# Prefix log-sum-exp in place: an fp32 work tile in three column chunks, row sums on VectorE, one fp32 product per chunk, and a range check

## The chip, the cores and the metric

The kernel runs on one core of one Trainium2 chip. The metric is the device time of one execution in microseconds (us). TensorE, VectorE, ScalarE and GpSimd appear in the profile as PE, DVE, ACT and POOL; SP is the engine that issues all transfers between DRAM and the core's memory (SBUF). PEld is TensorE's weight load, and a trailing q (SPq) means the engine's queue.

## The reference

The input x is a float32 array of 4 batches x 4096 rows x 4128 columns, drawn from a standard normal distribution. For each batch and each column the output is the running log-sum-exp down the rows:

```python
out[:, 0, :] = x[:, 0, :].copy()
for t in range(1, S):
    mx = np.maximum(out[:, t - 1, :], x[:, t, :])
    out[:, t, :] = mx + np.log(np.exp(out[:, t - 1, :] - mx) + np.exp(x[:, t, :] - mx))
```

So row t holds the logarithm of the sum of exp(x) over rows 0 to t. 270.5 MB are read and as many written.

## The kernel before

A **step** takes 128 x r consecutive rows of one batch, with r = 3 (or 2 where the 32 groups of 128 rows of a batch don't divide by three). Partition p holds rows p*r to p*r+r-1, so a step is one contiguous transfer of r rows per partition. There are 44 steps: 11 per batch, the step with r = 2 first in batch 0 and last in batches 1 to 3. Four work tiles (`xpool`, 4 buffers of 3 x 4128 float32 per partition) hold the steps. `Step.load` (L132) and `Step.store` (L135) are issued by SP and nothing else is; the result is written into the same work tile over the input.

A step is cut into 4 **chunks** of 1024 columns; the last chunk also carries the 32 columns that are left over, with small products and tiles of their own (`tail_head`, `qt`). What happens to a chunk:

- `exp` (L147, ACT) computes exp of its r rows as fp16, packed over the input's place in the work tile;
- `later` (L155, DVE) adds rows 1 and 2 into a float32r tile `sum`;
- `head` (PE) builds in PSUM the running sum at row 0 of each partition: an inclusive triangular product of row 0, an exclusive triangular product of the others (L167 for the float32r sum), and a `pick` product that adds the total of the step before out of `carry`;
- `stage(j)` takes the logarithm of PSUM into row j of the work tile (L198, ACT), then an identity product adds row j+1 to PSUM;
- after the last row `keep` (L111 and L112, DVE) saves the total as a high and a low fp16 part in `carry`.

The order of instructions on every engine is the order of the program text (`manual_schedule`), an order written out by hand. In turn g of the main loop the kernel issues `later` of chunk g+1, then the stages of chunks g-2, g-1 and g, then `exp` of chunk g+2 and `head` of chunk g+1. When the last stage of a step's last chunk is issued, SP gets that step's store and, right behind it, the load three steps ahead, which has to wait until the store before has left its tile:

```python
                if k.c == last and d + 1 == k.t.r:
                    k.t.store()
                    if bufs <= stored + ahead < len(steps):
                        steps[stored + ahead].load()
                    stored += 1
```

Of the kernel before, what the change touches and what calls it, by code (L numbers as in the profile page):

```python
# [6 lines left out]

FP32 = mybir.dt.float32
FP16 = mybir.dt.float16
FP32R = mybir.dt.float32r  # L10
ACT = mybir.ActivationFunctionType
P = 128
R = 3
CH = 1024
MM = 512
HI, LO = 96, 32


def _constants(nc, pool):


    def tri(base, name):
        t = pool.tile([P, P], FP16, name=name)
        nc.gpsimd.memset(t, 1.0)

        nc.gpsimd.affine_select(
            out=t, in_=t, pattern=[[1, P]], compare_op=mybir.AluOpType.is_ge,
            fill=0.0, base=base, channel_multiplier=-1,
        )
        return t  # L30

    def ones_where_zero(bases, step, name):
        t = pool.tile([P, P], FP16, name=name)
        nc.gpsimd.memset(t, 0.0)
        for base in bases:
            nc.gpsimd.affine_select(
                out=t, in_=t, pattern=[[step, P]], compare_op=mybir.AluOpType.not_equal,
                fill=1.0, base=base, channel_multiplier=1,
            )
        return t  # L40

    return (
        tri(0, "incl"),
        tri(-1, "excl"),
        ones_where_zero([0], -1, "ident"),
        ones_where_zero([-(HI + 31), -(LO + 31)], 0, "pick"),
    )


@with_exitstack  # L50
def kernel(
# [2 lines left out]
    x: bass.AP,  # L54
    out: bass.AP,
):

    nc = tc.nc
    B, S, D = x.shape
    assert S % P == 0
    n_main = D // CH
    tail = D - n_main * CH
    t0 = n_main * CH
    last = n_main - 1

    nc.scalar.preload_act_table_set("natural_log_exp_and_others")
    consts = ctx.enter_context(tc.tile_pool(name="consts", bufs=1))
    incl, excl, ident, pick = _constants(nc, consts)

    bufs = 4
    xpool = ctx.enter_context(tc.tile_pool(name="xpool", bufs=bufs))
    cpool = ctx.enter_context(tc.tile_pool(name="cpool", bufs=1))
    pmain = ctx.enter_context(tc.tile_pool(name="pmain", bufs=3, space=bass.MemoryType.PSUM))
    ptail = ctx.enter_context(tc.tile_pool(name="ptail", bufs=2, space=bass.MemoryType.PSUM))

    carry = [cpool.tile([P, CH], FP16, name=f"carry{c}") for c in range(n_main)]
    carry_t = cpool.tile([P, tail], FP16, name="carry_t")
    for t in (*carry, carry_t):
        nc.vector.memset(t, 0.0)

    spool = ctx.enter_context(tc.tile_pool(name="spool", bufs=1))
    excl_r = consts.tile([P, P], FP32R, name="excl_r")
    nc.vector.tensor_copy(excl_r, excl)

    ctx.enter_context(tc.manual_schedule())  # L90

    held = [None]

    def mm(pt, w, rhs, start=False, stop=False):

        if held[0] is not w:
            nc.tensor.matmul(pt, lhsT=w, rhs=rhs, start=start, stop=stop, skip_group_check=True)  # L97
            held[0] = w
            return
        pe = nc.tensor  # L100
        pe.add_instruction(mybir.InstMatmult(  # L101
            name=nc.get_next_instruction_name(),
            ins=[pe.lower_ap(rhs), pe.lower_ap(w, for_matmul_weights=True)],
            outs=[pe.lower_ap(pt, opt=True)],
            start_tensor_calc=start, stop_tensor_calc=stop, ldweights=False,
            tile_size=(P, P), tile_position=(0, 0), bass_skip_group_check=True,
        ))

    def keep(cr, pt):

        nc.vector.tensor_copy(cr[HI:HI + 32, :], pt[HI:HI + 32])  # L111
        nc.vector.tensor_tensor(  # L112
            out=cr[LO:LO + 32, :], in0=pt[HI:HI + 32], in1=cr[HI:HI + 32, :],
            op=mybir.AluOpType.subtract,
        )

    class Step:


        def __init__(self, b, row, r):  # L120
            self.b, self.row, self.r = b, row, r
            self.first = row == 0

        def dram(self, t):
            rows = t[self.b, self.row:self.row + P * self.r, :]
            return rows.rearrange("(p j) d -> p j d", j=self.r)

        def load(self):
            full = xpool.tile([P, R, D], FP32, name="xt")
            self.xt = full[:, :self.r, :]  # L130
            self.half = self.xt.bitcast(FP16)
            nc.sync.dma_start(out=self.xt, in_=self.dram(x))  # L132

        def store(self):
# [1 line left out]

    class Chunk:
        def __init__(self, step, c):
            self.t, self.c = step, c
            self.w = D - last * CH if c == last else CH  # L140

        def e(self, j, a, b):
            return self.t.half[:, j, 2 * self.c * CH + a:2 * self.c * CH + b]

        def exp(self):
            c0, w = self.c * CH, self.w
            nc.scalar.activation(  # L147
                self.t.half[:, :, 2 * c0:2 * c0 + w], self.t.xt[:, :, c0:c0 + w], ACT.Exp,
            )

        def later(self):

            if self.t.r == 3:
                self.sum = spool.tile([P, CH], FP32R, name="sum")
                nc.vector.tensor_tensor(  # L155
                    out=self.sum, in0=self.e(1, 0, CH), in1=self.e(2, 0, CH),
                    op=mybir.AluOpType.add,
                )

        def head(self):  # L160
            t = self.t
            pt = self.pt = pmain.tile([P, CH], FP32, name="pt")
            for s in range(0, CH, MM):
                mm(pt[:, s:s + MM], incl, self.e(0, s, s + MM), start=True)
            if t.r == 3:
                for s in range(0, CH, MM):
                    nc.tensor.matmul(  # L167
                        pt[:, s:s + MM], lhsT=excl_r, rhs=self.sum[:, s:s + MM],
                        start=False, stop=False, skip_group_check=True,
                    )  # L170
                held[0] = None
            else:
                for s in range(0, CH, MM):
                    mm(pt[:, s:s + MM], excl, self.e(1, s, s + MM))
            if not t.first:
                for s in range(0, CH, MM):
                    mm(pt[:, s:s + MM], pick, carry[self.c][:, s:s + MM])
            if self.c == last:
                self.tail_head()

        def tail_head(self):


            t, r = self.t, self.t.r
            full = ptail.tile([P, R, tail], FP32, name="qt")
            qt = self.qt = full[:, :r, :]
            to = lambda v, n: v.unsqueeze(1).to_broadcast([P, n, tail])
            for i in range(r):
                mm(qt[:, i:, :], incl, to(self.e(i, CH, CH + tail), r - i), start=i == 0)
            for i in range(1, r):  # L190
                mm(qt[:, :i, :], excl, to(self.e(i, CH, CH + tail), i))
            if not t.first:
                mm(qt, pick, to(carry_t, r))

        def stage(self, j):

            t, c, pt = self.t, self.c, self.pt
            nc.scalar.activation(t.xt[:, j, c * CH:(c + 1) * CH], pt, ACT.Ln)  # L198
            if j + 1 < t.r:
                for s in range(0, CH, MM):  # L200
                    mm(pt[:, s:s + MM], ident, self.e(j + 1, s, s + MM), stop=j + 2 == t.r)
                if c == last and j == 0:
                    nc.scalar.activation(t.xt[:, :, t0:D], self.qt, ACT.Ln)  # L203
                    keep(carry_t, self.qt[:, t.r - 1, :])
            else:
                keep(carry[c], pt)

    steps = []
    for b in range(B):
        n = S // P  # L210
        parts = [R] * (n // R) + ([n % R] if n % R else [])
        if b == 0:
            parts.reverse()
        row = 0
        for r in parts:
            steps.append(Step(b, row, r))
            row += P * r
        assert row == S

    chunks = [Chunk(s, c) for s in steps for c in range(n_main)]  # L220
    ahead = bufs - 1
    for s in steps[:bufs]:
        s.load()
    stored = 0
    chunks[0].exp()
    chunks[1].exp()
    chunks[0].later()
    chunks[0].head()
    for g in range(len(chunks) + R - 1):
        if g + 1 < len(chunks):  # L230
            chunks[g + 1].later()
        for d in range(R - 1, -1, -1):
            if 0 <= g - d < len(chunks) and d < chunks[g - d].t.r:
                k = chunks[g - d]
                k.stage(d)
                if k.c == last and d + 1 == k.t.r:
                    k.t.store()
                    if bufs <= stored + ahead < len(steps):
                        steps[stored + ahead].load()
                    stored += 1  # L240
        if g + 2 < len(chunks):
            chunks[g + 2].exp()
        if g + 1 < len(chunks):
            chunks[g + 1].head()


# [28 lines left out]
```

## Time and profile before

| | |
|---|---|
| time, median of 3 runs | 1262.85 us (1262.8 to 1263.05) |
| span of the profiled execution | 1261.5 us |
| busy: PE / DVE / ACT | 661.2 / 647.7 / 947.3 us (52% / 51% / 75%) |
| DMA | 541.44 MB, mean 429 GB/s over the span |
| mean granted TensorE clock | 0.722 |
| ACT waiting for a load (L147) | 248.4 us |

The profiled execution is listed with its span, from the first to the last instruction; the 1.35 us by which the median time is longer lie around the span. "Busy" is a share of the whole span. A group of instructions is listed with its count, its busy time, the mean duration of one in ns, and the idle time of the engine before it with what ended that idle time. Windows list busy time per engine in a stretch of the span, then the granted clock, the share of the 16 DMA engines' time in use, and GB/s.

### The profile page before, as it was taken

Reading aid. Unit: us, or ns where it says so; the run is one execution under the profiler, and the core shown is the slowest. Engines: PE = TensorE matmul, PEld = TensorE weight load, DVE = VectorE, ACT = ScalarE, POOL = GpSimd, SP = SyncE. Lnnn points to the kernel's source line nnn. Section 1 sums busy time; section 2 is a strip of 40 time slices with the busy share of each in tenths; the row PEclk is TensorE's granted clock in tenths of the full one; section 3 lists DMA queues with packets and bytes.
Section 4 is the critical chain, followed back from the end, with each engine's and each line's share of the span. In section 5 each row is a group of like instructions: output and inputs, shape, how many; then the busy total and the mean of one; then the engine's idle time right before and its main releaser. Section 6 shows DMA issues by size and latency. Waiting matters only on the chain. (4 is left out here: it accounts for less than half of the span.)

```text
span 1261.5 us, 5926 instructions
## 1 busy us (share of the span) xinstructions
PE 661.2 (52%) x1948; PEld 236.7 (19%) x1948; DVE 647.7 (51%) x606; ACT 947.3 (75%) x733; POOL 2.2 (0%) x13
## 2 busy tenths in 40 slices
PE   3655545465555555555446554555534655544562
PEld 1222111122121111211112121111111221111120
DVE  2674445554555545545446545544544645544454
ACT  5997777777777777778669777777866977777784
POOL 0000000000000000000000000000000000000000
PEclk9987676766577776768757677766775767787666
DMA  9999999999999999999999999999999999999998
GB/s 410 410 437 434 429 430 437 431 430 431 440 430 431 430 439 430 431 433 431 438 433 435 428 432 438 432 430 431 434 435 430 435 427 436 434 434 429 437 416 346
DMA packets 12702, 541.44 MB, mean 429 GB/s; under 512 B 1408, under 2 KB 1408, under 8 KB 1408
## 3 DMA queue, kind: packets, MB, share of 16 engines
q1 hardware_dynamic: 12672, 541.07, 99.4%
q8 instruction: 15, 0.25, 0.1%
q14 instruction: 15, 0.12, 0.0%
HBM read 270.53 MB, written 270.53 MB: 429 GB/s over the span
## 5 line engine op out<-in xcount | busy, mean ns | idle before, releaser
L147 ACT ACTIVATE xt<-xt 128x3072 f16<-128x3072 f32 (+3 forms) x176 | 478.3, 2717 | 248.4 <-DMA xt<-in_x_dram 248.4
L198 ACT ACTIVATE xt<-pt 128x1024 f32<-128x1024 f32 x512 | 487.5, 1029 | 2.5 <-PE pt L101 0.7
L155 DVE TENSOR_TENSOR sum<-xt 128x1024 fp32r<-128x1024 f16 x160 | 196.0, 1225 | 531.2 <-ACT xt L147 406.7
L97 PE MATMUL pt<-xt,ident 128*128 128x512 f16 x176 | 82.9, 471 | 482.8 <-ACT xt L198 482.8
L111 DVE CAST carry<-pt 32x1024 f16<-32x1024 f32 x176 | 216.4, 1230 | 46.4 <-ACT xt L198 41.3
L101 PE MATMUL pt<-xt,ident 128*128 128x512 f16 x496 | 209.5, 495 | 28.4 <-ACT xt L198 28.1
L112 DVE TENSOR_TENSOR carry<-pt,carry 32x1024 f16<-32x1024 f32 x176 | 215.9, 1226 | 6.1
L167 PE MATMUL pt<-sum,excl_r 128*128 128x512 f32 x320 | 198.7, 716 | 0.0
L101 PEld LDWEIGHTS <-ident 128*128 128x128 f16 x496 | 52.4, 106 | 646.5 <-issue 636.1
L97 PE MATMUL pt<-xt,incl 128*128 128x512 f16 x176 | 95.7, 544 | 71.7 <-DVE carry L112 54.0
L167 PEld LDWEIGHTS pt<-sum,excl_r 128*128 128x128 f32 x320 | 95.4, 298 | 48.4 <-issue 31.1
L101 PE MATMUL pt<-xt,incl 128*128 128x512 f16 x176 | 99.2, 564 | 0.0
L97 PE MATMUL pt<-carry,pick 128*128 128x512 f16 x160 | 84.4, 528 | 0.0
L101 PE MATMUL pt<-carry,pick 128*128 128x512 f16 x160 | 79.4, 496 | 0.0
L97 PEld LDWEIGHTS <-incl 128*128 128x128 f16 x220 | 23.7, 108 | 192.7 <-DVE carry L112 167.0
L203 ACT ACTIVATE xt<-qt 128x96 f32<-128x96 f32 (+1 forms) x44 | 10.9, 249 | 46.3 <-PE pt L101 46.3
L97 PEld LDWEIGHTS <-pick 128*128 128x128 f16 x200 | 24.2, 121 | 67.0 <-issue 66.3
L101 PEld LDWEIGHTS <-incl 128*128 128x128 f16 x260 | 27.6, 115 | 12.7 <-issue 9.2
L97 PEld LDWEIGHTS <-ident 128*128 128x128 f16 x176 | 21.4, 122 | 30.3 <-issue 24.3
L101 PEld LDWEIGHTS <-pick 128*128 128x128 f16 x160 | 20.5, 128 | 2.4 <-issue 1.7
L111 DVE CAST carry_t<-qt 32x32 f16<-32x32 f32 x44 | 8.7, 197 | 13.7 <-ACT xt L203 13.5
L97 PE MATMUL qt<-xt,incl 128*128 128x96 f16 (+1 forms) x44 | 10.6, 240 | 0.0
(25 smaller groups left out, 79.8 us busy)
## 6 DMA issues: line engine op xcount, KB each, us to landing
xt<-in_x_dram SPq DMA_DIRECT2D x40, 6192.0 KB, 42.3
out_dram<-xt SPq DMA_DIRECT2D x40, 6192.0 KB, 28.1
xt<-in_x_dram SPq DMA_DIRECT2D x4, 4128.0 KB, 37.4
out_dram<-xt SPq DMA_DIRECT2D x4, 4128.0 KB, 29.7
```

Source lines behind the costliest of these rows:

```text
L97: nc.tensor.matmul(pt, lhsT=w, rhs=rhs, start=start, stop=stop, skip_group_check=True)
L101: pe.add_instruction(mybir.InstMatmult(name=nc.get_next_instruction_name(), ins=[pe.lower_ap(rhs), pe.lower_ap(w, for_matmul_weights=True) ...
L111: nc.vector.tensor_copy(cr[HI:HI + 32, :], pt[HI:HI + 32])
L112: nc.vector.tensor_tensor(out=cr[LO:LO + 32, :], in0=pt[HI:HI + 32], in1=cr[HI:HI + 32, :], op=mybir.AluOpType.subtract,)
L147: nc.scalar.activation(self.t.half[:, :, 2 * c0:2 * c0 + w], self.t.xt[:, :, c0:c0 + w], ACT.Exp,)
L155: nc.vector.tensor_tensor(out=self.sum, in0=self.e(1, 0, CH), in1=self.e(2, 0, CH), op=mybir.AluOpType.add,)
L167: nc.tensor.matmul(pt[:, s:s + MM], lhsT=excl_r, rhs=self.sum[:, s:s + MM], start=False, stop=False, skip_group_check=True,)
L198: nc.scalar.activation(t.xt[:, j, c * CH:(c + 1) * CH], pt, ACT.Ln)
L203: nc.scalar.activation(t.xt[:, :, t0:D], self.qt, ACT.Ln)
```

## The change

- The columns are cut into 3 chunks of 1376; there are no left-over columns any more.
- `exp` writes float32 in place. The fp16 packing and the split of the carry are gone.
- `sums` (DVE) adds the r rows of a partition: for r = 3 row 1 becomes row 0 + row 1 in place, and row 1 + row 2 goes to a tile `z` (one per chunk, kept from step to step), on partitions 0 to 126 only. Partition 127 of `z` keeps the running total of the step before.
- `head` (PE) is one float32 product per chunk, in pieces of 512, 512 and 352 columns, with a triangular matrix whose last row is ones (`carried`), so that the total in partition 127 reaches every row; the first step of a batch uses `below`, without that row.
- `add` (DVE) adds the product to rows 0 to r-2 in place, and then makes the last row, which is also the new total, in `z`. `log` (ACT) takes the logarithm of rows 0 to r-2 in place, and of `z` into row r-1.
- The steps of a batch are 2, 3, 3, 3, 2, 3, 3, 3, 2, 3, 3, 2 groups: 48 steps instead of 44. Work tiles come from a pool of one tile with 2 rows and a pool of three tiles with 3 rows.
- A probe keeps the smallest exp of each batch's row 0 and the last totals (`tensor_reduce` in the first and last step of each batch). At the end the probe is compared with two limits, reduced to a flag, and a branch runs a general, row-by-row kernel (`_general`) if a value was out of range.
- The order of the main loop is new, and it differs at the end: `late` is true from the turn whose chunk g+2 lies in the last step.

```diff
         def exp(self):
-            c0, w = self.c * CH, self.w
-            nc.scalar.activation(
-                self.t.half[:, :, 2 * c0:2 * c0 + w], self.t.xt[:, :, c0:c0 + w], ACT.Exp,
+            e = self.t.xt[:, :, self.cols]
+            nc.scalar.activation(e, e, ACT.Exp)
+
+        def sums(self):
+            t, r = self.t, self.t.r
+            e = [t.xt[:, j, self.cols] for j in range(r)]
+            if t.first:
+                k = t.b * NC + self.c
+                nc.vector.tensor_reduce(
+                    out=probe[0:1, 1, k:k + 1], in_=e[0][0:1], op=ALU.min, axis=AX.X,
+                )
+            if r == 3:
+                nc.vector.tensor_tensor(out=e[1], in0=e[0], in1=e[1], op=ALU.add)
+            n = P - 1
+            nc.vector.tensor_tensor(
+                out=self.z[0:n], in0=e[r - 2][0:n], in1=e[r - 1][0:n], op=ALU.add,
             )
...
+        def head(self):
+            pt = self.pt = ppool.tile([P, CH], FP32, name="pt")
+            w = below if self.t.first else carried
+            for a, b in cuts:
+                nc.tensor.matmul(
+                    pt[:, a:b], lhsT=w, rhs=self.z[:, a:b], start=True, stop=True,
                 )
...
+        def add(self):
             t, r = self.t, self.t.r
...
+            e = t.xt[:, 0:r - 1, self.cols]
+            base = self.pt.unsqueeze(1).to_broadcast([P, r - 1, CH])
+            nc.vector.tensor_tensor(out=e, in0=base, in1=e, op=ALU.add)
+            nc.vector.tensor_tensor(
+                out=self.z, in0=t.xt[:, r - 2, self.cols], in1=t.xt[:, r - 1, self.cols],
+                op=ALU.add,
+            )
+            if t.last:
+                k = t.b * NC + self.c
+                nc.vector.tensor_reduce(
+                    out=probe[96:P, 0, k:k + 1], in_=self.z[96:P], op=ALU.add, axis=AX.X,
+                )
+
+        def log(self):
+            t, r = self.t, self.t.r
+            e = t.xt[:, 0:r - 1, self.cols]
+            nc.scalar.activation(e, e, ACT.Ln)
+            nc.scalar.activation(t.xt[:, r - 1, self.cols], self.z, ACT.Ln)
...
+    for g, k in enumerate(chunks):
+        nxt = chunks[g + 1] if g + 1 < n else None
+        far = chunks[g + 2] if g + 2 < n else None
+        late = far is None or far.t is steps[-1]
+        if not late:
+            far.exp()
+            nxt.sums()
+        k.add()
+        k.log()
+        if late:
+            if far:
+                far.exp()
+            if nxt:
+                nxt.sums()
+        if k.c == NC - 1:
+            k.t.store()
+            if bufs <= stored + ahead < len(steps):
+                steps[stored + ahead].load()
+            stored += 1
+        if nxt:
+            nxt.head()
...
+    wrong = nc.values_load(flag[0:1, 0:1], min_val=0, max_val=1)
+    with tc.If(wrong > 0):
+        _general(tc, x, out)
```

## The prediction

> **What bounds the kernel now.** I read the page first (busy shares and DMA), then the groups by shape, then ScalarE's timeline at the loads, and last windows and timelines of the end. A "group" below is 128 rows of all 4128 columns, 2.11 MB; a step of r rows moves r groups in and r out, 256 groups in all.
>
> ```profile
> DMA  9999999999999999999999999999999999999998
> DMA packets 12702, 541.44 MB, mean 429 GB/s; under 512 B 1408, under 2 KB 1408, under 8 KB 1408
> q1 hardware_dynamic: 12672, 541.07, 99.4%
> ```
>
> The DMA engines are in use from end to end, 99.4% on one queue, while ACT, the busiest engine, has 75%. The change moves the same bytes. So the stretch that could change is one where DMA doesn't run, or would stop running.
>
> ```profile
> 1167.16 2.76 ACT L147 ACTIVATE xt<-xt 128x3072 f16<-128x3072 f32 x1 [6.09 <-DMA xt<-in_x_dram]
> ...
> 1196.59 2.76 ACT L147 ACTIVATE xt<-xt 128x3072 f16<-128x3072 f32 x1 [6.16 <-DMA xt<-in_x_dram]
> ...
> 1221.49 1.91 ACT L147 ACTIVATE xt<-xt 128x2048 f16<-128x2048 f32 x1 [1.64 <-DMA xt<-in_x_dram]
> ```
>
> ACT's timeline: the first exp of a step starts 0.4 us after its load lands (the chain has the last landing at 1221.12). Between two landings the queue does one store and one load. Six groups take 29.4 us and five (the last load has r = 2) 24.9, and so do five elsewhere, nearly (882.65 to 907.22: 24.6). That is 4.90 us a group for long and short transfers alike, so four more steps cost nothing by themselves.
>
> ```profile
> 1225.00:1230.00 5.00, 4.09 (x10) 1.32 (x10) 2.19 (x4) 3.90 (x5) 0.00 (x0) 0.62 0.81 348
> 1230.00:1235.00 5.00, 3.51 (x10) 1.13 (x10) 2.68 (x3) 5.00 (x6) 0.00 (x0) 0.73 0.12 50
> 1235.00:1240.00 5.00, 2.59 (x10) 0.74 (x9) 4.87 (x5) 4.97 (x5) 0.00 (x0) 0.93 1.11 476
> ...
> 1245.00:1250.00 5.00, 0.00 (x0) 0.00 (x0) 2.71 (x4) 0.26 (x1) 0.00 (x0) 0.59 0.74 317
> ```
>
> Windows of the end (last three columns: clock, DMA share, GB/s): here alone DMA stops. The three missing shares (0.19, 0.88, 0.26 of 5 us) are 6.6 us. The stores of the last two steps wait for compute. After the last landing the end takes 1261.5 - 1221.1 = 40.4 us.
>
> ```profile
> L198 ACT ACTIVATE xt<-pt 128x1024 f32<-128x1024 f32 x512 | 487.5, 1029 | 2.5 <-PE pt L101 0.7 <-PE qt L97 0.3
> L147 ACT ACTIVATE xt<-xt 128x3072 f16<-128x3072 f32 x120 | 332.0, 2767 | 233.1 <-DMA xt<-in_x_dram 233.1
> L155 DVE TENSOR_TENSOR sum<-xt 128x1024 fp32r<-128x1024 f16 x160 | 196.0, 1225 | 531.2 <-ACT xt L147 406.7 <-PE pt L167 122.9 <-PE pt L101 1.6
> L167 PE MATMUL pt<-sum,excl_r 128*128 128x512 f32 x320 | 198.7, 716 | 0.0
> L167 PEld LDWEIGHTS pt<-sum,excl_r 128*128 128x128 f32 x320 | 95.4, 298 | 48.4 <-issue 31.1
> L111 DVE CAST carry_t<-qt 32x32 f16<-32x32 f32 x44 | 8.7, 197 | 13.7 <-ACT xt L203 13.5
> ```
>
> These give the prices. DVE: 32 elements 197 ns, 1024 elements 1225: 1.04 ns an element and 0.16 us. ACT: 3072 elements 2767 ns, 2048 (another form of L147) 1912: 0.835 ns and 0.20 us; L198 fits with 0.18.
>
> **The change: the middle.** For r = 3, ACT's exp of 4128 elements is 3.65 us, its two logarithms 2.5 and 1.3: 7.5 a chunk. DVE: `sums` 2 x 1.6 = 3.2, `add` 3.0 + 1.6 = 4.6: 7.8. For r = 2 ACT has 2.5 + 1.3 + 1.3 = 5.2, DVE 1.6 + 3.2 = 4.8. Summed over 96 long and 48 short chunks: DVE 980 us and 24 reductions of 1.6, ACT 970. DMA needs 6 x 4.90 / 3 = 9.8 a long chunk and 6.5 a short one. All fits below DMA. Removed are the casts and splits L111/L112 (432 us of DVE), L155, and most PE products: none of it ended a wait for DMA, so they are worth nothing here.
>
> The store must also reach the queue in time. By the order on the engines, store(s) follows, from the landing of s+1, one exp, a pair of logarithms, a second exp and a second pair: 3.65 + 3.85 + 3.65 + 3.85 + 0.4 = 15.4 us (about 17 before: 1196.2 to 1212.4 gives 16.2). Until then the queue holds store(s-1) and load(s+2): 4 groups at the least (steps 8 and 11 of a batch), else 5 or 6, that is 19.6 to 29.4 us. Margin 4 us at the tightest, once a batch, so DMA never stops. The load behind it waits for store(s-1), which lands about 15 us after the landing of s+1: even. `head` of chunk g+1 runs while DVE does `add`(g) and `sums`(g+2), 7.8 us of cover (4.8 in short steps); without this cover each product would stand on DVE's path. Start: store(0) has until 57 us, when four loads of 11 groups are through, and comes at about 41. The memsets on POOL (1376 elements each) are done long before the first landing at 12.8. Cost of the middle and start: 0, from -2 to +4.
>
> **The product's price.** No plain float32 product is in the trace. From below: as L167's float32r, two of which take 0.82 us at the clock of the end, so 0.41 x 1376/512 = 1.1 us a chunk. From above: a 24-bit significand cut in halves on both sides makes four partial products, each like one fp16 product:
>
> ```profile
> 1227.42 0.63 PE L101 MATMUL pt<-xt,incl 128*128 128x512 f16 x1
> 1227.85 0.63 PE L97 MATMUL pt<-xt,excl 128*128 128x512 f16 x1
> ...
> 1237.33 0.39 PE L97 MATMUL pt<-xt,incl 128*128 128x512 f16 x1
> 1237.55 0.38 PE L101 MATMUL pt<-xt,incl 128*128 128x512 f16 x1
> ```
>
> Starts are 0.43 us apart at the low clock and 0.22 at the full one; four of them over 1376 columns are 4.6 or 2.4 us. I take 4.0, nearer the low clock because the new PE works in bursts of 4 us with pauses of over 6 (the rows at 1227 follow pauses, those at 1237 an unbroken stretch), and 0.3 for weights (298 ns): H = 4.3. Ends: 1.1 and 4.9.
> The Trainium skill (FP8 and Floating Point Precision, TensorE Precision Notes) says true FP32 takes four passes through the array; no run here shows it yet, and by it the sum below would be 1284, by the L167 row 1272. The Trainium skill (TensorE: Matmul & The Clock Gate, Part 1) says the clock is at half rate by default and rises after about 3.4 us of sustained work; the two pairs of rows agree (0.43 and 0.22 us), and by it H is near its upper end.
>
> **The end.** Here the new order loses its overlap. From the turn where chunk g+2 is in the last step (`late`), `sums` of the next chunk stands behind `add` and its `head` behind that: sums, product and add of each chunk run one after another, with nothing between. Steps are 45 (r 3), 46 (r 3), 47 (r 2); the last two landings are 4 groups, 19.6 us, apart (store 44 and load 47). With a full DMA the last lands at 1221.1 as now, 46 at 1201.5. From there, in us:
> - DVE: sums(46,0) at 4.1 after its exp, add(45,2), sums(46,1), add(46,0) and add(46,1) without a pause: 4.1 + 3.2 + 4.6 + 3.2 + 4.6 + 4.6 = 24.3. ACT keeps pace (exp(46,2) ends at 18.9, store 45 at 15.4), and exp(47,0) runs at 26.6, after its landing.
> - From 24.3: sums(46,2) 3.2, H, add 4.6: 32.1 + H = 36.4. Store 46 follows its last logarithm, at 38.7.
> - Chunks (47,0) and (47,1): sums 1.6, H, add 3.2, reduction 1.6 (DVE goes on to the next sums only after it): 6.4 + H each, to 57.8.
> - (47,2): sums 1.6, H, add 3.2, logarithm 1.3, SP 0.4: store 47 at 51.4 + 4H = 68.6.
> - DMA has long stopped (store 46 ends at 38.7 + 14.7 = 53.4), so the 2 groups go alone: 9.8 + 1.2 (the store of before that queued for its data landed about 1 us behind it) = 11.0; end of span 0.9 after landing, as now (1260.6 to 1261.5); hand-overs between engines, some 20 of 0.05, 1.0.
>
> Span: 1201.5 + 68.6 + 11.0 + 0.9 + 1.0 = 1283.0; with the 1.35 us around it **1284.4**, or 1267.2 + 4H. The flag's few small DVE and PE operations, its read by every engine and the branch follow the last add, under the 11 us of the last store; uncovered they would cost up to 3. DMA would now stand still 9 us before store 46 and 15 before store 47, where 6.6 were lost.
>
> **The rivals.**
> (1) DMA starves in the middle. If the product isn't covered, a long chunk costs 3.2 + 4.3 + 4.6 = 12.1 against 9.8. It would decide from 9.8 us of DVE a chunk; the 24% margin and the order (two DVE operations between) speak against it, DVE's in-place float32 reads and writes beside full DMA, which no row shows, for a mild form: 1 us in each of the 32 long steps comes to 1316. Together 1293 to 1340: chance 0.09.
> (2) No change: the stores of the end still find DMA busy, or H is near nothing and DVE's operations overlap their hand-overs. Even H = 0 gives 1267, so it needs 4 us from elsewhere: 1261 to 1265, chance 0.05.
> (3) Faster: `late` lets store 46 go without waiting for two further chunks of step 47, and closes the 6.6 us gap: 1256 at the best. It decides if VectorE does two float32 elements a cycle, 0.85 us for 1.6: the serial part (25 us of DVE) then loses 13 us and, with H = 1.1, 13 more: 1258. L155 at 1.04 ns an element speaks against it. 0.03.
> (4) The check sends the data to the general path: 4095 rows in turn with a transfer each way, at over 4 us each, is above 16000 us. Sums of exp of normal values don't come near 2^62. Below 0.01.
>
> **How the numbers follow.** The forecast's case has 0.83: H from 1.1 to 4.9 is 1272 to 1287; hand-overs of 0.15 instead of 0.05 and the branch add up to 5: 1292. That range leaves out rivals (1) to (4) and the case's own edges, 2 in 10. A measurement here tells 0.2%, 2.5 us, from no change: faster 0.03, within 0.05, slower 0.92.
>
> **What would show it.** Right: the page's DMA row full up to the last slice or two and 0 or little in stretches of some 9 and 15 us in the last 50; the last landing within 3 us of 1221; PE rows of the product waiting for `sums` (DVE) and `add` waiting for PE in the last 45 us, and hardly before; four chunks with a product of about 4.3 us each. Wrong: landings more than 29.4 us apart for six groups in the middle (rival 1); store 47 issued before 1255 (rivals 2 and 3); a product of 1.1 us (low end).

## The result

| | before | after |
|---|---|---|
| time, median | 1262.82 us (1262.71 to 1263.05) | 1296.22 us (1293.67 to 1299.13) |
| span of the profiled execution | 1261.5 us | 1291.9 us (time of this execution 1293.67) |
| DMA share x span | 99.4% x 1261.5 = 1253.9 us | 97.6% x 1291.9 = 1260.9 us |

The changed kernel is slower by the ratio 1.0265 (95% interval 1.025 to 1.028), 33 us. The forecast was 1284.4, with 1272 to 1292. DMA share x span is the time that the packets of the main queue took, as a mean of the 16 DMA engines; the share is given to 0.1%, so the product is good to about 1.3 us. From the page of the changed kernel, its DMA and GB/s rows and its main queue, and then the GB/s row of the kernel before:

```profile
DMA  9999999999999999999999999999999999999964
GB/s 402 423 413 428 433 429 432 436 430 404 438 433 427 439 427 431 435 430 420 423 425 435 439 428 439 428 438 426 415 429 429 435 434 432 434 437 429 433 279 180
q1 hardware_dynamic: 13824, 541.07, 97.6%
```

```profile
GB/s 410 410 437 434 429 430 437 431 430 431 440 430 431 430 439 430 431 433 431 438 433 435 428 432 438 432 430 431 434 435 430 435 427 436 434 434 429 437 416 346
```

The last two slices are the end that the prediction is about. But there are also dents that the kernel before doesn't have: 413 in the third slice (65 to 97 us, where it has 437), 404 in the tenth, 420 in the 19th and 415 in the 29th. The last three lie where one batch gives way to the next. The packets of the same 541 MB took 7 us more of the engines' time. The DMA row shows 9 in all four places.

The end, in windows of the changed kernel (the last three columns are clock, DMA share and GB/s):

```profile
1240.00:1245.00 5.00, 0.00 (x0) 0.00 (x0) 4.97 (x3) 0.42 (x1) 0.00 (x0) 0.50 0.00 0
...
1250.00:1265.00 15.00, 5.47 (x8) 1.83 (x7) 9.18 (x6) 5.68 (x4) 0.00 (x0) 0.73 0.86 370
1265.00:1270.00 5.00, 1.25 (x2) 0.76 (x3) 3.54 (x3) 2.59 (x2) 0.00 (x0) 0.50 0.00 0
1270.00:1275.00 5.00, 2.75 (x5) 0.92 (x4) 2.17 (x2) 0.00 (x0) 0.00 (x0) 0.83 0.00 0
```

DMA stands still twice: in finer windows from about 1238.4 to 1248, and from 1264 to 1279. That is 10 and 15 us. Why it does is seen when the timelines of VectorE and TensorE are laid side by side (start, duration, and in brackets the idle time before and what ended it):

```profile
1239.84 3.02 DVE L121 TENSOR_TENSOR xt<-pt,xt 128x2752 f32<-128x2752 f32 x1 [5.11 <-PE pt L113]
1242.90 1.59 DVE L122 TENSOR_TENSOR z<-xt 128x1376 f32<-128x1376 f32 x1
1244.41 1.58 DVE L105 TENSOR_TENSOR z<-xt 127x1376 f32<-127x1376 f32 x1
1251.10 1.59 DVE L121 TENSOR_TENSOR xt<-pt,xt 128x1376 f32<-128x1376 f32 x1 [5.11 <-PE pt L113]
```

```profile
1234.87 4.93 PE L113 MATMUL pt<-z,carried 128*128 128x512 f32 x6 [7.96 <-DVE z L105]
1246.14 4.92 PE L113 MATMUL pt<-z,carried 128*128 128x512 f32 x6 [6.34 <-DVE z L105]
```

The product starts when `sums` (L105) ends, and `add` (L121) starts when the product ends: 1246.0, 1246.1, 1251.1. Each engine waits for the other. Over the whole page VectorE waits 20.9 us for TensorE; the waits of the last 67 us alone hold 19.5 of it:

```profile
ACT xt L135 <- DVE z L122: 26.5, 6, 8.1
...
DVE xt L121 <- PE pt L113: 19.5, 5, 5.1
```

The groups by shape give the new durations:

```profile
L113 PE MATMUL pt<-z,carried 128*128 128x512 f32 x528 | 440.9, 984 | 613.2 <-DVE z L105 613.2
L92 ACT ACTIVATE xt<-xt 128x4128 f32<-128x4128 f32 x96 | 348.7, 3632 | 207.7 <-DMA xt<-in_x_dram 207.7
L121 DVE TENSOR_TENSOR xt<-pt,xt 128x2752 f32<-128x2752 f32 x96 | 289.7, 3018 | 5.7 <-PE pt L113 5.7
L105 DVE TENSOR_TENSOR z<-xt 127x1376 f32<-127x1376 f32 x144 | 228.9, 1590 | 17.8 <-ACT xt L92 13.8
```

VectorE and ScalarE are as worked out (3.02, 1.59 and 3.63 us against 3.0, 1.6 and 3.65). A chunk's three pieces are six matmul instructions, so a float32 piece takes two.

### The profile page after: what moved, and what is told of

It reads as the page before. It is cut to its first block, busy times and chain, and to the rows that moved or that the text cites. A ratio compares the mean times of both kernels' runs of the same rounds, so it can differ in the third digit from the quotient of the medians.

```text
span 1291.9 us, 3364 instructions
## 1 busy us (share of the span) xinstructions
PE 605.4 (47%) x866; PEld 236.8 (18%) x866; DVE 996.0 (77%) x556; ACT 937.3 (73%) x433; POOL 4.6 (0%) x12
## 3 DMA queue, kind: packets, MB, share of 16 engines
q1 hardware_dynamic: 13824, 541.07, 97.6%
## 5 line engine op out<-in xcount | busy, mean ns | idle before, releaser
L113 PE MATMUL pt<-z,carried 128*128 128x512 f32 (+1 forms) x792 | 557.9, 867 | 613.2 <-DVE z L105 613.2
L92 ACT ACTIVATE xt<-xt 128x4128 f32<-128x4128 f32 (+1 forms) x144 | 467.7, 3249 | 240.3 <-DMA xt<-in_x_dram 240.3
L113 PEld LDWEIGHTS pt<-z,carried 128*128 128x128 f32 x792 | 218.0, 293 | 952.4 <-issue 952.4
L121 DVE TENSOR_TENSOR xt<-pt,xt 128x2752 f32<-128x2752 f32 (+1 forms) x144 | 365.6, 2539 | 20.9 <-PE pt L113 20.9
L135 ACT ACTIVATE xt<-xt 128x2752 f32<-128x2752 f32 (+1 forms) x144 | 303.8, 2109 | 100.3 <-DVE z L122 99.7
L103 DVE TENSOR_TENSOR xt<-xt 128x1376 f32<-128x1376 f32 x96 | 152.3, 1587 | 216.4 <-ACT xt L92 216.3
L105 DVE TENSOR_TENSOR z<-xt 127x1376 f32<-127x1376 f32 x144 | 228.9, 1590 | 17.8 <-ACT xt L92 13.8
L122 DVE TENSOR_TENSOR z<-xt 128x1376 f32<-128x1376 f32 x144 | 229.3, 1593 | 4.9
L136 ACT ACTIVATE xt<-z 128x1376 f32<-128x1376 f32 x144 | 192.0, 1333 | 0.0
L113 PE MATMUL pt<-z,below 128*128 128x512 f32 (+1 forms) x72 | 47.3, 817 | 54.4 <-DVE z L105 54.4
## 6 DMA issues: line engine op xcount, KB each, us to landing
out_dram<-xt SPq DMA_DIRECT2D x16, 4128.0 KB, 26.4
```

The lines of the kernel that those rows point to most:

```text
L92: nc.scalar.activation(e, e, ACT.Exp)
L103: nc.vector.tensor_tensor(out=e[1], in0=e[0], in1=e[1], op=ALU.add)
L105: nc.vector.tensor_tensor(out=self.z[0:n], in0=e[r - 2][0:n], in1=e[r - 1][0:n], op=ALU.add,)
L113: nc.tensor.matmul(pt[:, a:b], lhsT=w, rhs=self.z[:, a:b], start=True, stop=True,)
L121: nc.vector.tensor_tensor(out=e, in0=base, in1=e, op=ALU.add)
L122: nc.vector.tensor_tensor(out=self.z, in0=t.xt[:, r - 2, self.cols], in1=t.xt[:, r - 1, self.cols], op=ALU.add,)
```

## The experiments

Theory A: the end is a chain of `sums`, product and `add`, because of the late order. Rival B: most is lost in the middle. When the dents had been seen, theory M was added for those at the change of batch: at the short pair (a store of 2 groups and, three steps on, a load of 2 groups) the queue runs short, and packets take longer afterwards. Its rival N: short transfers, or more of them, cost time as such. All times are medians, set against 1296.2 for the changed kernel, whose own runs spread over 5 us; differences of 2 or 3 us are not settled by them.

**1. Early order at the end.**

```diff
-        late = far is None or far.t is steps[-1]
+        late = False
         if not late:
-            far.exp()
-            nxt.sums()
+            if far:
+                far.exp()
+            if nxt:
+                nxt.sums()
```

> Edit: late is always False, so the next chunk's sums and the exp of the chunk after it stand ahead of add to the last turn. Theory A (the end is a chain of sums, product and add, one after another, because of the late order): in the profile of the changed kernel the last store is issued 71.8 us after the landing of step 46; with the early order sums and add cover the product again and it comes at about 52.5, so 19 us less: time about 1277 (1274 to 1281), and the pauses of DMA of about 8 and 16 us shrink to about 2 in all. Theory B (the 33 us are mostly lost in the middle, where packets take longer and DMA is short of work): 5 us less at most, time above 1290. The middle (DMA share times span, 1261 us) stays in both.

Measured: 1278.6 us (1278.0 to 1280.9), 17.6 less. Its waits from 1225 on, to be compared with those above:

```profile
PE pt L113 <- DVE z L105: 12.6, 5, 3.4
ACT xt L135 <- DVE z L122: 7.7, 5, 2.7
```

`add` no longer appears as waiting for PE at all. Step 46 lands at 1214.2 and the last store is issued at 1266.0: 51.8 us, nearly as worked out, against 71.5 in the changed kernel (1207.2 to 1278.7; the 71.8 of the expectations puts the landing 0.35 us too early, as the next section shows). One pause of DMA is left, of some 6 us by the shares of these windows, where about 2 were expected:

```profile
1245.00:1250.00 5.00, 2.90 (x6) 1.16 (x5) 4.78 (x4) 5.00 (x3) 0.00 (x0) 0.84 0.05 20
1250.00:1255.00 5.00, 3.20 (x5) 1.01 (x3) 4.90 (x4) 5.00 (x4) 0.00 (x0) 0.67 0.74 317
```

Theory A holds for somewhat more than half of the loss. In this execution the landing of step 46 came 7 us later than in the changed kernel's, though the instructions up to there are the same ones: the middle differs from execution to execution. Counted from this landing to the end of the span, 65.0 us are left of 84.7, which is 19.7 less.

**2. Only exp late.**

```diff
         if not late:
             far.exp()
+        if nxt:
             nxt.sums()
         k.add()
         k.log()
-        if late:
-            if far:
-                far.exp()
-            if nxt:
-                nxt.sums()
+        if late and far:
+            far.exp()
```

> Edit: the late order is kept for exp alone; sums goes ahead of add to the last turn. Theory A: the product is covered by add again, but sums of step 47 now wait for exps that stand behind the logarithms; worked out from the profile's durations the last store comes about 61.5 us after the landing of step 46, 10 us less than the changed kernel: time about 1286 (1282 to 1290). If exp's place is what costs, nothing changes (1296); if only sums behind add costs, it is as with the early order (1277).

Measured: 1293.1 us (1290.1 to 1295.1), 3 less and not clearly different. A miss: the wait only changed its place.

```profile
1240.63 1.59 DVE L105 TENSOR_TENSOR z<-xt 127x1376 f32<-127x1376 f32 x1 [6.25 <-ACT xt L92]
...
1253.03 1.59 DVE L105 TENSOR_TENSOR z<-xt 127x1376 f32<-127x1376 f32 x1 [6.25 <-ACT xt L92]
```

VectorE doesn't wait for the product now but, for 6.25 us each time, for an exp that ScalarE gets to only behind the logarithms of the chunk before, which wait for `add`. Both halves of the late order have to go together.

**3. A product in float32r.** `z` and the weights become float32r tiles, so the sums are rounded before the product.

```diff
-    z = [zpool.tile([P, CH], FP32, name=f"z{c}") for c in range(NC)]
+    z = [zpool.tile([P, CH], FP32R, name=f"z{c}") for c in range(NC)]
...
-            w = below if self.t.first else carried
+            w = below_r if self.t.first else carried_r
```

> Edit: z and the triangular weights are float32r instead of float32, so the sums are rounded before the product; the rest as in the changed kernel. Theory A: the product of a chunk falls from 4.9 us to about 1.3 to 1.8 (three pieces like the float32r rows of the kernel before), and four of them stand in the chain of the end: 12 to 14 us less, time 1282 to 1284. If the product is hidden at the end: 1296. In the middle nothing changes in either: DMA share times span stays at about 1261 us.

Measured: 1282.1 us (1281.6 to 1284.3), 14.2 less, as theory A says. One instruction per piece is left, and a shorter one:

```profile
L120 PE MATMUL pt<-z,carried_r 128*128 128x512 f32 x264 | 157.3, 697 | 964.0 <-DVE z L112 964.0
```

DMA share x span stays at 98.5% x 1281.0 = 1261.8: the product's price matters at the end and nowhere else.

**4. No short pair.** The last two steps of batches 0 to 2 change places, so that the lengths end ...3, 2, 3.

```diff
+        if b + 1 < B:
+            parts[-2:] = parts[:-3:-1]
```

> Edit: in batches 0 to 2 the last two steps change places (2 then 3 groups), so that no store and the load three steps on are both short; the queue then holds at least 5 groups (24.5 us) while a store is waited for, instead of 4 (19.6). Theory M (at the short pair the faster DMA engines run dry, restart together and then packets take longer; 1.1, 1.4 and 0.8 us were lost at the three places): DMA share times span falls from 1261 us to 1256 to 1258, time 3 to 5 us less, 1291 to 1293. Theory N (short transfers, or 48 instead of 44 of them, cost time as such): 1261 us and 1296 as before. The end is the same.

Measured: 1290.1 us (1289.4 to 1291.5), 6.1 less, and the spread of the runs falls from 5.5 to 2.2 us. DMA time is 97.6% x 1288.1 = 1257.2 us, 3.7 less for the same bytes and the same 96 transfers. The three dents at the change of batch (tenth, 19th and 29th slice) are gone; the one in the third slice is not:

```profile
GB/s 402 422 407 428 427 427 434 428 441 429 434 432 430 435 433 429 437 432 429 435 434 434 433 435 430 437 431 434 427 441 430 428 439 429 439 430 435 417 277 181
```

Windows around the short pair of batch 0, first the changed kernel, then this one:

```profile
270.00:276.00 6.00, 4.83 (x6) 1.72 (x6) 5.93 (x4) 5.25 (x3) 0.00 (x0) 0.58 1.01 435
276.00:278.50 2.50, 0.91 (x2) 0.49 (x3) 2.50 (x2) 2.50 (x3) 0.00 (x0) 0.98 0.86 370
278.50:284.00 5.50, 3.22 (x5) 1.01 (x3) 5.43 (x4) 5.08 (x2) 0.00 (x0) 0.70 1.01 435
```

```profile
276.00:278.50 2.50, 2.50 (x4) 1.06 (x5) 2.46 (x2) 0.64 (x1) 0.00 (x0) 0.65 1.14 495
```

In the changed kernel the store of step 9 is issued at 278.18, when the fastest of the 16 DMA engines is about to run out of work: it is through with the load before this store at 278.44, the slowest at 282.43. The share falls to 0.86. Here the same store is issued at 271.79, and the fastest engine is through with the load before it only at 279.88. The trace's landings of the single engines fit: in the changed kernel there are 4.0 us between the first and the last of the 16 before this store and 2.7 after it, because the faster ones had to wait. The idle time itself is only about 0.4 us for an engine on average; the larger part is lost afterwards, when the engines are nearer to each other and some of their packets take up to about 1 us longer than the 1.83 or 1.22 of their kind elsewhere (such packets lie at 291.8 and 302 us, and likewise at the next two changes of batch). Between 250 and 350 us longer packets add 1.9 us for an engine, here 0.5. Theory N is refuted; why these packets are slower, and whether working in step is the reason, stays open.

**5. Early order and no short pair.** Both edits together.

> Edit: both the early order at the end and the exchange of the last two steps in batches 0 to 2. Theory: the two losses are separate, so the gains add: 17.6 (early order) and 6.1 (no short pair) off 1296.2: 1272.5 (1270 to 1275). If the exchange helped only because the chain of the end began earlier, or the early order only by chance of the middle, the sum falls short: 1276 or more.

Measured: 1269.3 us (1267.8 to 1271.2), 26.9 less; the parts alone gave 17.6 + 6.1 = 23.7. They add up and a little more, within the spread of the changed kernel. DMA time is 99.2% x 1267.6 = 1257.5. So the two executions without the short pair have 1257.2 and 1257.5 us, and the five with it (the changed kernel and experiments 1, 2, 3 and 8) 1260.9 to 1263.8; the share is given to 0.1%, which is 1.3 us.

**6. Steps of two groups in five tiles**, with the early order:

```diff
-    x2 = ctx.enter_context(tc.tile_pool(name="x2", bufs=1))
-    x3 = ctx.enter_context(tc.tile_pool(name="x3", bufs=3))
+    x2 = ctx.enter_context(tc.tile_pool(name="x2", bufs=5))
...
+        parts = [2] * (n // 2)
...
-    bufs, ahead, stored = 4, 3, 0
+    bufs, ahead, stored = 5, 4, 0
```

> Edit: early order, and all steps are 2 groups (64 steps) in five work tiles of 2 rows, loads four steps ahead. Theory M: while a store is waited for (10.8 us after the landing of the next step: two exps of 2.5, two pairs of logarithms of 2.7, 0.4) the queue holds 6 groups, 29.4 us, so DMA never runs dry, in the middle or at the end (8 groups of stores are left after the last landing, the last store is issued 26 us after it): DMA share times span 1254 to 1258, no pause at the end, time 1262 to 1267. Theory N (each transfer more, or each short one, costs, by what the changed kernel lost: 7 us for 8 more or 32 short ones): 128 short transfers give 20 to 35 us of DMA time, time above 1280.

Measured: 1265.1 us (1263.9 to 1265.7), ratio to the kernel before 1.0018 (1.0009 to 1.0027). Its main queue:

```profile
q1 hardware_dynamic: 18432, 541.07, 99.5%
```

128 short transfers need 99.5% x 1262.5 = 1256.2 us, less than the 96 of the changed kernel: theory N is wrong by 18 us or more, and with 29 us of work in the queue DMA is busy from end to end.

**7. The same with four tiles** (`bufs=4`, loads three steps ahead).

> Edit: as the one with five tiles, but with four and loads three steps ahead. Theory M: the queue holds 4 groups (19.6 us) against a store after 10.8 us: margin 8.8 where the changed kernel had 4 at its tightest, so the middle is as good as with five tiles (DMA share times span 1254 to 1258); at the end 6 groups are left, the last store comes 26 us after the last landing (about 1231) and adds 12: time 1269 to 1272. Theory N: above 1285. If depth of the queue alone counts and not the margin, DMA share times span is as in the changed kernel, 1261.

Measured: 1280.6 us (1279.9 to 1281.3): 9 us above the upper end of theory M. DMA time is 98.4% x 1279.6 = 1259.1 us, also above the 1254 to 1258 that it gave. The end was as expected (the last store 26.4 us after the last landing at 1238.7), but that landing came 8 us late, and the GB/s row says where:

```profile
GB/s 405 372 408 427 422 432 433 427 432 431 433 431 430 435 432 435 432 431 434 435 433 430 432 433 437 430 430 432 436 433 429 428 434 433 432 432 435 435 363 265
```

The second and third slice are low: the four loads and the first store are through by 52 us, the second store comes too late, and DMA runs dry (that store lands 5 us late). From the fourth slice on the rate is even. The margin that I worked out holds for the steady part, and I had not applied it to the start.

**8. The last reductions moved** behind the last `add`:

```diff
-            if t.last:
+            if t.last and t is not steps[-1]:
...
+    for k in chunks[-NC:]:
+        i = k.t.b * NC + k.c
+        nc.vector.tensor_reduce(
+            out=probe[96:P, 0, i:i + 1], in_=k.z[96:P], op=ALU.add, axis=AX.X,
+        )
```

> Edit: the late order as in the changed kernel; the three reductions of the last step's totals stand behind its last add instead of behind each add. Two of them (1.6 each) stood in the chain of the end: the last store is issued 3.3 us earlier after the landing of step 46 (68.5 instead of 71.8), time 1293 (1290 to 1296). If the reductions ran beside the product: no change of these 71.8 us.

Measured: 1293.9 us (1292.4 to 1297.3), 2.3 less, inside the spread; from the landing of step 46 to the last store 68.8 us instead of 71.5. The product took part of the 3.3 back: `add` of the last three chunks waited 5.07 to 5.11 us each time here, and 5.11, 4.59 and 4.19 in the changed kernel.

**9 and 10. Stores by chunk at the end.** Both have the early order and the reductions moved, and the last two steps are stored in three parts each. The first has no short pair, the second has steps of two groups in five tiles.

```diff
+        if k.t in steps[-2:]:
+            nc.sync.dma_start(out=k.t.dram(out)[:, :, k.cols], in_=k.t.xt[:, :, k.cols])
+        elif k.c == NC - 1:
-        if k.c == NC - 1:
             k.t.store()
```

> Edit: early order, no short pair, the last step's reductions behind its last add, and the last two steps stored chunk by chunk (six stores of 1376 columns instead of two). Theory: after the last landing only DMA's own work is left: the first part of step 46 leaves about 14 us after the landing of 46, so DMA no longer pauses before store 46 (4 us in the version without this), and the last store is a third as long: 4 to 5 us less than early order and exchange alone (1269.3), 1264 to 1266. If short rows (5.5 KB pieces) slow the transfers down, or the end is bound by the slowest DMA engine anyway: 1268 or more.

> Edit: 64 steps of 2 groups in five tiles with the early order, the last reductions deferred and the last two steps stored chunk by chunk. Theory: DMA is already busy up to the last store there, so the end is bound by the slowest DMA engine, and this changes little: 1263 to 1265.1. If the last store still came late for the faster engines only, the same; if the end is bound by compute after all, 3 to 6 us less, 1259 to 1262.

Measured: 1266.7 us (1264.9 to 1266.9) and 1266.0 us (1265.5 to 1267.3). The first gains 2.7 on the kernel with early order and exchange alone, less than was expected, the second nothing. Ratios to the kernel before are 1.0029 (1.0018 to 1.0039) and 1.0026 (1.0015 to 1.0036): no version tried is faster than the kernel before.

## Why the prediction was wrong

The side was right, and so was the mechanism of the end; the term for the middle and the start was wrong, and with it the size. Set against the prediction's sum, the profiled execution has 1291.9 - 1283.0 = 8.9 us of span more, in three of its terms:

- **"Cost of the middle and start: 0, from -2 to +4".** This step failed. Step 46 landed 5.7 us late, at 1207.2 against 1201.5, and the last step at 1226.7, outside the 3 us around 1221 that the prediction named as its sign:

```profile
1207.25 3.64 ACT L92 ACTIVATE xt<-xt 128x4128 f32<-128x4128 f32 x1 [7.69 <-DMA xt<-in_x_dram]
```

"Margin 4 us at the tightest, once a batch, so DMA never stops" named the place and drew the wrong end from it: it took the 16 engines for one. At the short pair of batch 0 the slowest engine did have 4.2 us (282.4 less 278.2), but the fastest had 0.3. The prediction's own rows could have shown that the engines drift apart: after the last landing of the kernel before, at 1221.1, 14.7 us of store were still queued, yet the DMA share was down to 0.12 between 1230 and 1235. The fastest engine was through with that store at 1228.3, the slowest at 1236.0. Without the short pairs step 46 lands at 1203.6 (experiment 4), so 3.6 of the 5.7 us are theirs in the profiled executions (6.1 us between the medians). The other 2.1 fit the dent in the third slice, which is there in experiments 4, 5 and 9 as well (407, 415 and 404). For the start the prediction had checked store 0 alone; store 1 was issued at 66.1, 1 us before the queue was through with store 0 at 67.2. No run changed the start alone, so this part is not shown.
- **The chain, 68.6 + 1.0 of hand-overs: 71.5 measured**, 1.9 more. H was 4.9, 4.9, 4.4 and 4.0 and not 4.3, and `add` waited 0.2 us more than that for each: 19.0 us in place of 17.2. Behind the last `add` the sum has one logarithm of 1.3, but both stood in the chain, 2.7 us, because the first one overwrites the row that the last addition (L122) reads and so waits for it:

```profile
1276.10 1.35 ACT L135 ACTIVATE xt<-xt 128x1376 f32<-128x1376 f32 x1 [8.06 <-DVE z L122]
1277.36 1.33 ACT L136 ACTIVATE xt<-z 128x1376 f32<-128x1376 f32 x1
```

Against that, the hand-overs came to almost nothing, and the 0.4 of SP belongs to the next term. Four partial products at the low clock was the right reading: a piece of 512 columns is two instructions of about 0.85 us there, four times the 0.43 of an fp16 product. The Trainium skill (FP8 and Floating Point Precision, TensorE Precision Notes) has four passes for true FP32, and the trace agrees. With the clock rule that was cited (The Trainium skill, TensorE: Matmul & The Clock Gate, Part 1) it agrees roughly: each of these four products began at a granted clock of 0.50, behind a pause of 6.3 to 8.0 us, and the clock rose to 1.00 at 1251.2, 1261.5 and 1271.7, that is 5.1, 3.8 and 2.9 us after the second, third and fourth had begun; for the first it didn't rise at all. So the first two took 4.93 and 4.92 us at the low clock, while the third and fourth were still running when it rose and took 4.41 and 4.00.
- **The last store to the end of the span: 13.2 measured**, 11.9 in the sum.

The landing itself needs a word, since "the first exp of a step starts 0.4 us after its load lands" was read from the last step alone. At the other steps on the chain of the kernel before it is 0.02 to 0.08 us: the load of step 41 lands 42.47 us after 1124.67, at 1167.14, and its exp starts at 1167.16. In the changed kernel step 46 lands 0.02 us before its exp, at 1207.23.

```profile
1124.67 42.47 DMA xt<-in_x_dram
```

To this come 0.4 us around the span (1.77 instead of 1.35) and 2.55 by which the median lies above the profiled execution: 8.9 + 0.4 + 2.6 = 11.8, the distance of 1296.2 from 1284.4. The prediction took for granted that executions agree as closely as before (0.3 us); they spread over 5.5, and in experiment 4 over 2.2.

**The range** had a fault of its own: its upper end was made of H and the hand-overs, and the +4 that the text gave to the middle was left out. With it the end is 1296, just short of the measured 1296.2.

Right were: the order of the chain, chunk by chunk; DMA's pauses of 9 and 15 us (10 and 15 measured); the prices of VectorE and ScalarE; that more transfers cost next to nothing as such (64 each way took 1256.2 us of DMA time in experiment 6, 2.3 more than the 44 of the kernel before); that the product is covered in the middle (VectorE waits 1.4 us for it up to 1225). Rival 1 was near in one point, that DMA is short of work in the middle, but by another mechanism: no chunk takes longer than DMA needs, only the queue is too short at some places. Rivals 2, 3 and 4 did not happen.

## What to carry to other kernels

When a kernel is bound by transfers, work out for each step how many us of transfers are queued when it waits for the next store, at the worst pair of step lengths and at the start, and take off what the fastest DMA engine is ahead of the slowest. Then follow the end instruction by instruction: an order that brings one store forward can take away the cover between two engines, and every product then counts in full. If two instructions were moved together, moving back one alone may only pass the wait on to another engine.

## What was not expected of the hardware

DMA packets are not equally long: with a queue that runs short at the start and once a batch the same 541.07 MB took 1260.9 us of the engines' time instead of 1253.9, and 1257.2 once the short pairs were gone. In the share of the DMA row a slow packet counts as busy; only share times span, or GB/s by slice, shows it. The 16 engines also drift apart, to 7.7 us between the first and the last landing of one transfer at the end of the kernel before; there the fastest engine had been out of work for 6.4 us when the next store was issued at 1234.8, and the slowest (1236.0) not at all. So the late engines hide a pause of the others, and the early ones take the margin away where the queue is short.
